# Three groups behind a layer norm: two corrected, the third on chunks normed in advance

## The chip, the cores and the metric

The kernel runs on one core of one Trainium2 chip. A core has a matrix engine (TensorE, PE in the profile), a vector engine (DVE), an activation engine (ACT), a general engine (POOL, GpSimd) and an engine that only issues transfers here (SP). Each works through its own list of instructions in order, and waits on semaphores for the others. The metric is device time in microseconds; lower is better.

## The reference, cut to what matters

Two layers transform a residual stream `h` of L = 272 rows (256 tokens and 16 meta rows) by D = 2048 features. Each layer is

```
proj = h @ w_in                      # q,k,v,gate for gated linear attention (GLA); q,k,v for neighbourhood attention
mix  = concat(gla(...), na(...)) @ w_out
h    = layer_norm(ALPHA * h + mix, ln1_w, ln1_b)
ff   = square(relu(h @ w_ff1)) @ w_ff2        # 2048 -> 8192 -> 2048
h    = layer_norm(ALPHA * h + ff, ln2_w, ln2_b)
layer_norm(x) = (x - mean) * rsqrt(var + eps) * gain + bias     # over the 2048 features of a row
```

The meta rows are dropped at the end, so the second layer needs only n = 256 rows behind its attention. Three norms are followed by a matrix product: the first norm of both layers (before `w_ff1`) and the second norm of layer 0 (before the `w_in` of layer 1, whose first columns are k and then v).

## The kernel before, in words

Activations lie transposed: 16 chunks `x[0..15]` of 128 features by L columns. Each chunk is a pair (high part, low part), two reduced-precision numbers that add up to the float; a product is then three matmuls: high weights by high x, high weights by low x, low weights by high x (`three`, lines 159 to 161). With n = 256 the first two are one matmul of 512 columns (lines 155 and 156).

Weights are streamed in tiles of 128 x 1024. `made` issues the transfer of a tile on SP into `raw`, casts it on ACT into `wh` (line 146) and subtracts on DVE into `wl` (line 147). All three have three buffers, and a tile is made one ahead of its use. One tile serves 8 chunks of one output of 128 features, or 2 chunks of four outputs.

A group is four outputs (512 columns of a weight matrix), that is eight tiles. `by_m` makes a group output by output: 16 chunks into one PSUM bank, then its evacuation. `by_k` makes it chunk by chunk: two chunks at a time into all four banks of the pool `pm`, so chunks may come late or may be overwritten behind it, but the four outputs end together. The host lays out the tiles of a group for one form or the other (`tiles`, `kinds`).

Behind a norm the mean and the scale of a row are known late. So `ln_add` writes into x the not yet normed value times the gain, and two more columns with gain and bias. A group on that x has n + 2 columns, and its sums are corrected by `fix` (lines 865 to 878): DVE copies the two extra sums out of PSUM (`wb`, line 874), subtracts mean times the gain's sum (line 875, which frees the bank), multiplies by the scale `rs` (line 876), and the evacuation adds the bias's sum as it applies its function. Meanwhile `ln_all` norms the accumulator `acc` itself, two chunks a step: two operations of DVE on both chunks (line 850, subtract and multiply), then gain and bias on POOL for each chunk (line 840). `renew` splits a normed chunk into x (lines 205 on ACT and 206 on DVE).

In the kernel before, both the first and the second group behind a norm are corrected. The first is `by_m`. The second is `by_k`, and behind each pair of chunks that it has used, `renew(k)` overwrites the pair before with normed values, for which it takes steps of `ln_all` where these are missing. From the third group on x is normed. In layer 0 and layer 1 the groups are the first two of `w_ff1`; between the layers they are k and v of layer 1.

Two queues of generators are worked off between the matmuls, by `pump(fg, bg)` after every 8 chunks: `fg` holds evacuations in pieces, `bg` holds `ln_all` (and GLA's heads). `NORMS = 0.4` is the number of `ln_all` steps a pump takes. A scheduler lays the instructions of each engine in one fixed order, in which such work is put behind the newest weight tile's `wl`.

The residual sum starts in `mixed`: POOL adds the two parts of each x chunk into `acc` (line 284) while the first group of `w_out` runs. In layer 1, v is evacuated by `ev_v` (line 362) and turned by three transposes (`v_rows`, line 371); the pool `early` that follows takes the memory of the norm's pools, and its first transfers (line 300 `wraw`, line 305 `wlr`) stand in SP's list among the weight tiles.

Of the kernel before, what the change touches and what calls it, by code (L numbers as in the profile page):

```python
# [14 lines left out]
P = 128  # L15
D = 2048
DC = D // P
# [14 lines left out]
EPS = 1e-5  # L32
TAU = 16.0
NEG = -1e30
GLA_R, GLA_NA, NORMS = 1.3, 1.1, 0.4


class Pair(tuple):
# [8 lines left out]
class Trunk:  # L47
# [138 lines left out]
                                      start=j + p == 0, stop=j == nk - 1 and p == 2)  # L186
        return [p[:, :n] for p in ps]

    def by_m(self, acts, ns, evict, pump=(0, 0), apart=False):

        nk = len(acts)
        for m, n in enumerate(ns):
            ps = self.pm.tile([P, 512], F32, name="mm", tag="mm")
            for k in range(nk):
                if k % 8 == 0:
                    wh, wl = self.weights()
                self.three(ps, wh, wl, (k % 8) * P, acts[k], n, k == 0, k == nk - 1)
                if k % 8 == 7 and k < nk - 1:
                    self.pump(*pump)
            parts = [ps[:, :T], ps[:, T:]] if n == T else [ps[:, :n]]  # L200
            evict(m, parts if apart else self.whole(parts))
            self.pump(*pump)
# [16 lines left out]
    def layer(self, l):  # L219
        nc, tc = self.nc, self.tc  # L220
        self.l = l
        self.full = l + 1 < DEPTH
        self.n = n = L if self.full else T
        with ExitStack() as actx:
            pool = lambda name, side, ctx=actx, bufs=1: ctx.enter_context(
                tc.tile_pool(name=name, bufs=bufs, side=side, reuse_waits="tile"))
            a = pool("att", "left")
            t = lambda nm, s: a.tile(s, F32, name=nm, tag=nm)
            self.qk = [t(f"qk{h}", [P, 2, L]) for h in range(GH)]
            self.be = [t(f"be{h}", [P, 2, L + 1]) for h in range(GH)]  # L230
            self.V = [t(f"V{i}", [P, GH * GDV]) for i in range(2)]
            self.VS = a.tile([80, GH * GDV], F32R, name="VS", tag="VS")
            nc.gpsimd.memset(self.VS.bitcast(F32), 0.0)
            self.y, self.gate, self.done = [None] * DC, {}, set()
            if l:
                self.by_m(self.x, [L + 2] * 4, lambda m, ps: self.fixed(self.ev_k, m, ps), pump=(1, NORMS))
                ps = self.by_k(self.x, L + 2, self.renew)
                self.renew(DC)
                for m in range(4):
                    self.fixed(self.ev_v, m, ps[m])  # L240
                self.drain()
                self.lctx.close()
            else:
                with ExitStack() as ectx:
                    self.xr = pool("xr", "right", ectx)
                    for m, ps in enumerate(self.by_k(self.x, L, self.load_x, fine=True)):
                        self.ev_k(m, ps)
            with ExitStack() as ectx:
                self.ep = pool("early", "right", ectx)
                self.fcredit = 0  # L250
                self.fg.append(self.gates())
                if l == 0:
                    self.by_m(self.x, [L] * 4, self.ev_v, pump=(1, 0))
                self.by_m(self.x, [n] * 4, self.ev_q, pump=(1, 0))
                self.by_m(self.x, [L] * 4, lambda m, ps: self.ev_v(4 + m, ps), pump=(1, 0))
                self.drain()
            self.a2 = pool("na", "left", bufs=2)
            with ExitStack() as gctx:
                self.credit = 0
                self.g2 = pool("gla", "right", gctx, 2)  # L260
                for h in range(GH):
                    self.bg.append(self.gla_head(h))
                for g in range(2):
                    self.by_m(self.x, [n] * 4, lambda m, ps: self.ev_r(4 * g + m, ps), pump=(1, GLA_R))
                self.na_tiles()
                for g in range(6):
                    if g == 5:
                        while self.bg:
                            self.step(self.bg, 1)
                        gctx.close()  # L270
                        self.ln_open()
                    ns = [n if (4 * g + m) % 3 == 0 else L for m in range(4)]
                    self.by_m(self.x, ns, lambda m, ps: self.ev_na(4 * g + m, ps), pump=(1, GLA_NA))
            ps = self.by_k(self.y, n, self.mixed)
            self.drain()
        self.tail(ps)

    def mixed(self, k):
        self.pump(1, 0)
        while not self.done.issuperset((k, k + 1)):  # L280
            self.step(self.fg, 1)
        for c in (k, k + 1):
            h, lo = (t[:, :self.n].bitcast(F32) for t in self.x[c])
            self.nc.gpsimd.tensor_tensor(self.acc[:, c, :self.n], h, lo, ALU.add)

    def load_x(self, k):
        nc = self.nc
# [68 lines left out]
    def ev_k(self, m, ps, **how):  # L356
        self.nc.scalar.activation(self.qk[m][:, 1, :], ps, AF.Identity, **how)

    def ev_v(self, c, ps, **how):
        pool, bufs = (self.l3, 3) if how else (self.ep, 2)  # L360
        vt = pool.tile([P, L], F32, name="ft", tag="ft", bufs=bufs)
        self.nc.scalar.activation(vt, ps, AF.Identity, **how)
        self.fg.append(self.v_rows(c, vt))

    def v_rows(self, c, vt):
# [296 lines left out]
    def tail(self, ps):  # L662
# [3 lines left out]
        with tc.tile_pool(name="u", bufs=1, reuse_waits="tile") as up:  # L666
# [6 lines left out]
            for half in range(2):  # L673
                u = [self.pair(self.yp, "y", k) if k < DC else self.pair(up, "u", k) for k in range(2 * DC)]

                def ev_f(k, ps, **how):
                    h, lo = u[k]
                    t = self.l3.tile([P, L], F32, name="ft", tag="ft")[:, :n]
                    if how or n > T:
                        nc.scalar.activation(t, ps, AF.Relu, **how)  # L680
                        nc.vector.tensor_tensor(t, t, t, ALU.mult)
                    else:
                        nc.vector.scalar_tensor_tensor(t, ps, 0.0, ps, ALU.max, ALU.mult)
                    self.split(t, h[:, :n], lo[:, :n])

                for g in range(8):
                    if half or g > 1:
                        self.by_m(self.x, [n] * 4, lambda m, ps: ev_f(4 * g + m, ps), pump=(1, 0))
                    elif g:
                        ps = self.by_k(self.x, n + 2, self.renew)  # L690
                        self.renew(DC)
                        for m in range(4):
                            self.fixed(ev_f, 4 + m, ps[m])
                        self.step(self.fg, 2)
                    else:
                        self.by_m(self.x, [n + 2] * 4, lambda m, ps: self.fixed(ev_f, m, ps), pump=(1, NORMS))

                def ev_2(m, ps, g):
                    k = 4 * g + m
                    a = acc[:, k, :n]  # L700
                    if half == 0:
                        nc.vector.scalar_tensor_tensor(a, a, ALPHA, ps[0], ALU.mult, ALU.add)
                        for part in ps[1:]:
                            nc.vector.tensor_tensor(a, a, part, ALU.add)
                    else:
                        self.ln_part(k, 1, ps)

                for g in range(4):
                    self.by_m(u, [n] * 4, lambda m, ps: ev_2(m, ps, g),
                              pump=(1, 0), apart=True)  # L710
# [102 lines left out]
    def ln_norm(self, which, l, n):  # L813
# [11 lines left out]
        nc.scalar.copy(mu, p1)  # L825
        nc.vector.tensor_tensor(var, p2, tn, ALU.subtract)
        end = self.newton(rs, var, self.eps, tn)
        self.norm = dict(mu=mu, rs=rs, last=end, n=n, ready=0, gb=[self.affine(l, which, k) for k in range(DC)])
        if not which or l < DEPTH - 1:
            self.bg.append(self.ln_all())  # L830
        yield
# [1 line left out]
    def ln_all(self):  # L833
        nc, acc, n = self.nc, self.acc, self.norm["n"]
        for k in range(0, DC, 2):
            self.ln_wide(k, 2, 0)
            self.ln_wide(k, 2, 1)
            for c in (k, k + 1):
                a, (gain, bias) = acc[:, c, :n], self.norm["gb"][c]
                nc.gpsimd.tensor_scalar(a, a, gain, bias, ALU.mult, ALU.add)  # L840
            self.norm["ready"] = k + 2
            yield

# [5 lines left out]
        by, alu = ((f["mu"], ALU.subtract), (f["rs"], ALU.mult))[op]  # L849
        return self.nc.vector.tensor_tensor(v, v, by[:, None, :].to_broadcast([P, m, n]), alu)  # L850

    def renew(self, k):

        f = self.norm
        n = f["n"]
        for c in (k - 2, k - 1) if k else ():
            while f["ready"] <= c:
                self.step(self.bg, 1)
            h, lo = self.x[c]
            self.split(self.acc[:, c, :n], h[:, :n], lo[:, :n])  # L860

    def fixed(self, evict, m, ps):
        self.fg.append(self.fix(evict, m, ps))
# [40 lines left out]
def layout(inputs):  # L904
# [28 lines left out]
    o["win"] = tiles(np.concatenate(cols, axis=2), ((0, 0), (1, 1)))  # L933
    o["wlr"] = lr.reshape(DEPTH, DC, P, 32).transpose(0, 2, 1, 3).reshape(DEPTH, P, 512)
    o["wout"] = tiles(a["w_out"], ((0, 0), (1, 0)))
    o["wff1"] = tiles(a["w_ff1"], ((0, 1), (1, 1)))
    o["wff2"] = tiles(a["w_ff2"], (), 2)
    wup = np.zeros((DEPTH, LRK, 2, GH * GDK), f)
    for s in range(0, 96, 32):
# [55 lines left out]
```

## Time and profile before

| | us |
|---|---|
| median of 3 runs (2457.91 to 2458.53) | 2458.18 |
| profiled execution | 2458.56 |
| its span | 2456.7 |
| PE busy in it | 2412.8 (98%) |
| DVE busy | 1581.8 (64%) |
| ACT busy | 1177.2 (48%) |
| POOL busy | 321.4 (13%) |

Matmuls overlap: a row of the timeline with 0.29 us is followed by the next after 0.127 us. What counts for the time is the distance of starts, and the idle time in brackets behind a row, with what ended it. PEclk is the granted clock of the matrix engine as a share of full speed.

### The profile page before, as it was taken

The numbers are of one execution on the slowest core, as the hardware profiler recorded it, in microseconds if no ns is written. First come the engines' busy times: TensorE is split into PE (matmuls) and PEld (weight loads), VectorE is DVE, ScalarE is ACT, GpSimd is POOL, SyncE is SP. The second block draws the span as 40 slices with busy tenths as digits, with TensorE's granted clock in tenths as the row PEclk, the third lists the DMA queues.
The fourth block names the chain that finished last, engine by engine and source line by source line (L and its number), as shares of the span: only waits on it lengthen the run. The fifth ranks groups of instructions, "written<-read, shape, count | busy, mean of one in ns | idle before, by whom it ended". The sixth has DMA issues, their size and how long they took to land.

```text
span 2456.7 us, 43382 instructions
## 1 busy us (share of the span) xinstructions
PE 2412.8 (98%) x17388; PEld 2261.3 (92%) x17388; DVE 1581.8 (64%) x2481; ACT 1177.2 (48%) x1938; POOL 321.4 (13%) x503
## 2 busy tenths in 40 slices
PE   9999999999999999999999999999899999999997
PEld 8999899999999999999998888898888888888886
DVE  6687777785544455546568787768866555666655
ACT  6555555454433344444446555555544333444443
POOL 1164340020000000000012444320300000000000
PEclk9999999999999999999999999999999999999998
DMA  7544444545555555555554444446465655555553
GB/s 239 162 135 144 137 136 155 174 153 176 176 173 177 174 174 178 172 175 175 174 184 149 147 152 154 134 155 198 152 192 188 189 188 187 185 187 188 187 189 129
DMA packets 118361, 417.25 MB, mean 170 GB/s; under 512 B 13388, under 2 KB 16460, under 8 KB 118160
## 3 DMA queue, kind: packets, MB, share of 16 engines
q1 hardware_dynamic: 118160, 414.49, 53.4%
q8 instruction: 136, 2.23, 0.4%
q14 instruction: 65, 0.53, 0.1%
HBM read 412.34 MB, written 2.10 MB: 169 GB/s over the span
## 4 chain that ended last, share of the span: by engine, by line
PE 92%; DVE 3%; POOL 2%; issue 1%; ACT 1%; DMA 0%; SPq 0%; ACTq 0%; POOLq 0%; DVEq 0%
PE mm L155 22%; PE mm L159 17%; PE mm L161 17%; PE mm L160 17%; PE mm L156 11%; PE mm L185 3%; POOL lev L455 1%; DVE acc L850 1%; POOL acc L840 1%; PE bg L490 1%; DVE wl L147 1%; PE bg L640 0%; PE bg L592 0%; PE bg L642 0%; ACT wh L146 0%
## 5 line engine op out<-in xcount | busy, mean ns | idle before, releaser
L147 DVE TENSOR_TENSOR wl<-raw,wh 128x1024 fp32r<-128x1024 f32 (+1 forms) x772 | 948.7, 1230 | 636.8 <-ACT wh L146 629.7
L146 ACT CAST wh<-raw 128x1024 fp32r<-128x1024 f32 (+1 forms) x772 | 806.2, 1045 | 944.3 <-PE mm L160 408.6
L159 PE MATMUL mm<-x,wh 128*128 128x272 f32 (+2 forms) x2112 | 615.4, 291 | 5.0 <-DVE wb L874 5.0
L161 PE MATMUL mm<-x,wl 128*128 128x272 f32 (+2 forms) x2112 | 610.5, 289 | 0.0
L160 PE MATMUL mm<-x,wh 128*128 128x272 f32 (+2 forms) x2112 | 610.3, 289 | 0.0
L155 PE MATMUL mm<-x,wh 128*128 128x512 f32 x1216 | 436.3, 400 | 10.6 <-DVE fx L875 10.6
L159 PEld LDWEIGHTS mm<-x,wh 128*128 128x128 f32 x2112 | 401.6, 190 | 9.6 <-ACT x L205 5.2
L161 PEld LDWEIGHTS mm<-x,wl 128*128 128x128 f32 x2112 | 398.8, 189 | 0.0
L160 PEld LDWEIGHTS mm<-x,wh 128*128 128x128 f32 x2112 | 398.2, 189 | 0.0
L156 PE MATMUL mm<-x,wl 128*128 128x256 f32 x1216 | 344.8, 284 | 1.0 <-DVE wl L147 1.0
L155 PEld LDWEIGHTS mm<-x,wh 128*128 128x128 f32 x1216 | 231.6, 190 | 66.2 <-ACT x L205 6.4
L155 PE MATMUL mm<-y,wh 128*128 128x512 f32 x704 | 247.9, 393 | 0.0
L156 PEld LDWEIGHTS mm<-x,wl 128*128 128x128 f32 x1216 | 231.5, 190 | 1.9 <-DVE wl L147 1.7
L161 PE MATMUL mm<-y,wl 128*128 128x272 f32 x704 | 203.1, 288 | 0.0
L159 PE MATMUL mm<-y,wh 128*128 128x272 f32 x704 | 203.0, 288 | 0.0
L160 PE MATMUL mm<-y,wh 128*128 128x272 f32 x704 | 202.7, 288 | 0.0
L156 PE MATMUL mm<-y,wl 128*128 128x256 f32 x704 | 197.5, 281 | 0.6 <-DVE wl L147 0.6
L155 PE MATMUL mm<-u,wh 128*128 128x512 f32 x512 | 180.6, 393 | 0.0
L455 POOL TENSOR_TENSOR lev<-be 128x128 f32<-128x128 f32 (+1 forms) x256 | 154.7, 634 | 143.7 <-PE bg L490 61.0
L155 PEld LDWEIGHTS mm<-y,wh 128*128 128x128 f32 x704 | 131.8, 188 | 30.1
L159 PE MATMUL mm<-u,wh 128*128 128x272 f32 x512 | 147.7, 288 | 0.0
L161 PE MATMUL mm<-u,wl 128*128 128x272 f32 x512 | 147.7, 288 | 0.0
(241 smaller groups left out, 3317.6 us busy)
## 6 DMA issues: line engine op xcount, KB each, us to landing
raw<-in_wff SPq DMA_DIRECT2D x512, 512.0 KB, 3.5
raw<-in_win SPq DMA_DIRECT2D x190, 512.0 KB, 3.6
raw<-in_wout SPq DMA_DIRECT2D x64, 512.0 KB, 3.6
nb<-in_nab SPq DMA_DIRECT2D x16, 352.0 KB, 3.2
out<-acc SPq DMA_DIRECT2D x8, 256.0 KB, 2.2
xraw<-in_xT SPq DMA_DIRECT2D x7, 272.0 KB, 5.4
wraw<-in_wup SPq DMA_DIRECT2D x2, 392.0 KB
raw<-in_win SPq DMA_DIRECT2D x4, 128.0 KB, 2.6
```

Source lines behind the costliest of these rows:

```text
L146: nc.scalar.copy(wh[:, c], raw[:, c])
L147: self.wl = nc.vector.tensor_tensor(wl[:, c], raw[:, c], wh[:, c].bitcast(F32), ALU.subtract).ins
L155: mm(ps, lhsT=wh[:, c:c + P], rhs=x.both[:, :, :T], start=first, stop=False)
L156: mm(ps[:, T:], lhsT=wl[:, c:c + P], rhs=xh[:, :T], start=False, stop=last)
L159: mm(o, lhsT=wh[:, c:c + P], rhs=xh[:, :n], start=first, stop=False)
L160: mm(o, lhsT=wh[:, c:c + P], rhs=xl[:, :n], start=False, stop=False)
L161: mm(o, lhsT=wl[:, c:c + P], rhs=xh[:, :n], start=False, stop=last)
L185: self.nc.tensor.matmul(ps[m][:, :n], lhsT=parts[p][0][:, c:c + P], rhs=acts[j][parts[p][1]][:, :n], start=j + p == 0, stop=j == nk - 1 an ...
L455: tt = lambda o, x, y: nc.gpsimd.tensor_tensor(o, x, y, ALU.subtract)
L490: nc.tensor.matmul(ps[b * 64:b * 64 + 64, s * 64:s * 64 + 64], lhsT=k[:, c:c + 64], rhs=q[:, r:r + 64], start=True, stop=True)
L840: nc.gpsimd.tensor_scalar(a, a, gain, bias, ALU.mult, ALU.add)
L850: return self.nc.vector.tensor_tensor(v, v, by[:, None, :].to_broadcast([P, m, n]), alu)
```

## The change

1. Behind each of the first norms of both layers, groups 0 and 1 of `w_ff1` are both `by_m` with corrected sums. `NORMS` becomes 0.6 there and 1.0 in front of k. At the middle of the last output before the third group, `renew(2)` norms the first two chunks.
2. Group 2 of `w_ff1` is `by_k` on normed x without the extra columns. Before each pair of chunks `normed(k)` takes one `fg` step and has chunks up to k + 4 split (`LEAD = 4`). Its four outputs are evacuated one a step through `later`. The host lays out group 2 for `by_k` instead of group 1.
3. Between the layers, k stays corrected and `by_m`; v becomes such a `by_k` on normed x with L columns instead of L + 2. Its outputs are evacuated after the norm's pools are closed, by plain copies on ACT, and their transposes go into the queue behind the decay gates instead of being run off before q.
4. `ln_all` gives gain and bias of the even chunks to ACT; the odd ones stay on POOL.
5. The corrected evacuation squares on ACT instead of DVE. Group 2 in layer 1 takes relu on ACT and the square on DVE, as layer 0 does.
6. `mixed` adds on DVE instead of POOL.

```diff
-GLA_R, GLA_NA, NORMS = 1.3, 1.1, 0.4
+GLA_R, GLA_NA, NORMS = 1.3, 1.1, (1.0, 0.6)
+LEAD = 4
...
+                if renew and m == len(ns) - 1 and k == 8:
+                    self.renew(2)
...
-                self.by_m(self.x, [L + 2] * 4, lambda m, ps: self.fixed(self.ev_k, m, ps), pump=(1, NORMS))
-                ps = self.by_k(self.x, L + 2, self.renew)
-                self.renew(DC)
-                for m in range(4):
-                    self.fixed(self.ev_v, m, ps[m])
+                self.by_m(self.x, [L + 2] * 4, lambda m, ps: self.fixed(self.ev_k, m, ps), pump=(1, NORMS[0]),
+                          renew=True)
+                first = self.by_k(self.x, L, self.normed)
                 self.drain()
                 self.lctx.close()
...
+                else:
+                    for m, ps in enumerate(first):
+                        self.ev_v(m, ps)
...
-            self.nc.gpsimd.tensor_tensor(self.acc[:, c, :self.n], h, lo, ALU.add)
+            self.nc.vector.tensor_tensor(self.acc[:, c, :self.n], h, lo, ALU.add)
...
-    def ev_v(self, c, ps, **how):
-        pool, bufs = (self.l3, 3) if how else (self.ep, 2)
-        vt = pool.tile([P, L], F32, name="ft", tag="ft", bufs=bufs)
-        self.nc.scalar.activation(vt, ps, AF.Identity, **how)
+    def ev_v(self, c, ps):
+        vt = self.ep.tile([P, L], F32, name="ft", tag="ft", bufs=4)
+        self.nc.scalar.copy(vt, ps)
...
-                    if how or n > T:
+                    if how:
                         nc.scalar.activation(t, ps, AF.Relu, **how)
+                        nc.scalar.activation(t, t, AF.Square)
+                    elif n > T or not half and 7 < k < 12:
+                        nc.scalar.activation(t, ps, AF.Relu)
                         nc.vector.tensor_tensor(t, t, t, ALU.mult)
...
-                    if half or g > 1:
+                    if half or g > 2:
                         self.by_m(self.x, [n] * 4, lambda m, ps: ev_f(4 * g + m, ps), pump=(1, 0))
-                    elif g:
-                        ps = self.by_k(self.x, n + 2, self.renew)
-                        self.renew(DC)
-                        for m in range(4):
-                            self.fixed(ev_f, 4 + m, ps[m])
-                        self.step(self.fg, 2)
+                    elif g == 2:
+                        ps = self.by_k(self.x, n, self.normed)
+                        self.fg.extend(self.later(ev_f, 8 + m, ps[m]) for m in range(4))
+                        self.step(self.fg, 1)
                     else:
-                        self.by_m(self.x, [n + 2] * 4, lambda m, ps: self.fixed(ev_f, m, ps), pump=(1, NORMS))
+                        self.by_m(self.x, [n + 2] * 4, lambda m, ps: self.fixed(ev_f, 4 * g + m, ps),
+                                  pump=(1, NORMS[1]), renew=g == 1)
...
-                nc.gpsimd.tensor_scalar(a, a, gain, bias, ALU.mult, ALU.add)
+                if c % 2:
+                    nc.gpsimd.tensor_scalar(a, a, gain, bias, ALU.mult, ALU.add)
+                else:
+                    nc.scalar.activation(a, a, AF.Identity, bias=bias, scale=gain)
...
-    def renew(self, k):
+    def normed(self, k):
+
+        self.pump(1, 0)
+        self.renew(min(DC, k + LEAD))
+
+    def renew(self, end):
 
         f = self.norm
         n = f["n"]
-        for c in (k - 2, k - 1) if k else ():
+        for c in range(f["new"], end):
             while f["ready"] <= c:
                 self.step(self.bg, 1)
             h, lo = self.x[c]
             self.split(self.acc[:, c, :n], h[:, :n], lo[:, :n])
+        f["new"] = end
+
+    def later(self, evict, m, ps):
+        evict(m, ps)
+        yield
...
-    o["wff1"] = tiles(a["w_ff1"], ((0, 1), (1, 1)))
+    o["wff1"] = tiles(a["w_ff1"], ((0, 2), (1, 2)))
```

More of the change, by code (lines that the diff above doesn't have):

```diff
@@ L187, in by_k, with by_m @@
         return [p[:, :n] for p in ps]
-    def by_m(self, acts, ns, evict, pump=(0, 0), apart=False):
+    def by_m(self, acts, ns, evict, pump=(0, 0), apart=False, renew=False):
         nk = len(acts)
@@ L827, in ln_norm @@
         end = self.newton(rs, var, self.eps, tn)
-        self.norm = dict(mu=mu, rs=rs, last=end, n=n, ready=0, gb=[self.affine(l, which, k) for k in range(DC)])
+        self.norm = dict(mu=mu, rs=rs, last=end, n=n, ready=0, new=0, gb=[self.affine(l, which, k) for k in range(DC)])
         if not which or l < DEPTH - 1:
```

## The prediction

> **What bounds the kernel now.** First the page's busy shares, then the view of waits for the matrix engine.
>
> ```profile
> span 2456.7 us, 43382 instructions
> ...
> PE 2412.8 (98%) x17388; PEld 2261.3 (92%) x17388; DVE 1581.8 (64%) x2481; ACT 1177.2 (48%) x1938; POOL 321.4 (13%) x503
> ```
> ```profile
> PE mm L155 <- DVE fx L875: 10.6, 2, 6.3
> PE mm L159 <- DVE wb L874: 5.0, 1, 5.0
> ```
>
> PE is busy for 98%, so only idle time and a lowered clock can be won. Three waits, 15.6 us together (10.6 + 5.0), end with the correction of an output, which frees a PSUM bank. Each lies at the end of the second corrected group, and the timeline of PE shows what each costs.
>
> ```profile
> 523.47 0.29 PE L185 MATMUL mm<-x,wh 128*128 128x274 f32 x1
> 528.77 0.56 PE L159 MATMUL mm<-x,wh 128*128 128x272 f32 x1 [5.02 <-DVE wb L874]
> ...
> 533.61 0.29 PE L159 MATMUL mm<-x,wh 128*128 128x272 f32 x1
> 533.74 0.29 PE L160 MATMUL mm<-x,wh 128*128 128x272 f32 x1
> ```
> ```profile
> 1304.61 0.29 PE L185 MATMUL mm<-x,wh 128*128 128x274 f32 x1
> 1309.21 0.77 PE L155 MATMUL mm<-x,wh 128*128 128x512 f32 x1 [4.32 <-DVE fx L875]
> ...
> 1316.16 0.39 PE L155 MATMUL mm<-x,wh 128*128 128x512 f32 x1
> ...
> 1317.09 0.49 PE L371 MATMUL bg<-ident,ft 128*128 128x128 f32 x3
> 1317.34 0.36 PE L156 MATMUL mm<-x,wl 128*128 128x256 f32 x1
> ...
> 1318.95 0.40 PE L155 MATMUL mm<-x,wh 128*128 128x512 f32 x1
> 1320.33 0.39 PE L156 MATMUL mm<-x,wl 128*128 128x256 f32 x1 [0.98 <-DVE wl L147]
> ```
> ```profile
> 1754.74 0.28 PE L185 MATMUL mm<-x,wh 128*128 128x258 f32 x1
> 1761.27 0.77 PE L155 MATMUL mm<-x,wh 128*128 128x512 f32 x1 [6.25 <-DVE fx L875]
> ...
> 1765.83 0.40 PE L155 MATMUL mm<-x,wh 128*128 128x512 f32 x1
> ...
> 1766.19 0.40 PE L155 MATMUL mm<-x,wh 128*128 128x512 f32 x1
> ...
> 1766.54 0.39 PE L155 MATMUL mm<-x,wh 128*128 128x512 f32 x1
> ```
>
> Behind each wait the starts are wider apart for a while: the granted clock is lower, as the windows show.
>
> ```profile
> 525.00:530.00 5.00, 1.23 (x5) 1.26 (x6) 4.20 (x11) 2.54 (x6) 3.55 (x4) 0.67 0.37 105
> ...
> 1310.00:1315.00 5.00, 5.00 (x18) 4.16 (x18) 3.86 (x14) 2.43 (x5) 0.03 (x1) 0.50 0.56 177
> ...
> 1320.00:1325.00 5.00, 4.67 (x31) 4.23 (x32) 4.67 (x7) 2.06 (x3) 0.00 (x0) 1.00 0.61 211
> ...
> 1760.00:1765.00 5.00, 3.73 (x11) 3.22 (x12) 4.51 (x12) 2.86 (x6) 1.16 (x2) 0.50 0.09 14
> ```
>
> The last three columns are the granted clock, the share of the transfer engines and GB/s. The clock is 0.50 to 0.67. So each place costs its wait and its slow stretch:
>
> - Layer 0, `w_ff1`: the next start was due at 523.47 + 0.13 = 523.60 and came at 528.77: 5.2. Then 21 matmuls took 4.84 (to 533.61) instead of 21 x 0.127 = 2.67: 2.2. Together 7.3.
> - Between the layers: due 1304.74, came 1309.21: 4.5. Up to 1316.16 there are 9 pairs of matmuls and three sets of transposes; at the later distances (0.352 a pair, 1766.19 to 1766.54; 0.25 a set, 1317.09 to 1317.34) that is 3.9, it took 6.95: 3.0. The row at 1320.33 came 1.38 behind its neighbour instead of two thirds of a pair, 0.24: 1.1. Together 8.6.
> - Layer 1, `w_ff1`: due 1754.86, came 1761.27: 6.4; 7 pairs in 4.56 instead of 2.46: 2.1. Together 8.5.
>
> Sum 24.4 us, all that can be won here. Why the bank comes late is seen in layer 0's second product:
>
> ```profile
> 1293.36 0.72 DVE L850 TENSOR_TENSOR acc<-acc,mu 128x544 f32<-128x544 f32 x1
> ...
> 1294.34 0.72 DVE L850 TENSOR_TENSOR acc<-acc,rs 128x544 f32<-128x544 f32 x1
> 1294.98 1.22 DVE L147 TENSOR_TENSOR wl<-raw,wh 128x1024 fp32r<-128x1024 f32 x1
> 1297.13 0.44 DVE L206 TENSOR_TENSOR x<-acc,x 128x272 fp32r<-128x272 f32 x1 [0.93 <-ACT x L205]
> 1297.49 0.72 DVE L850 TENSOR_TENSOR acc<-acc,mu 128x544 f32<-128x544 f32 x1
> ```
> ```profile
> 1295.23 1.96 POOL L840 TENSOR_SCALAR acc<-acc,vec 128x272 f32<-128x272 f32 x2 [2.17 <-DVE acc L850]
> ```
>
> Two chunks run through DVE, POOL, ACT and DVE again, one pair every 1297.49 - 1293.36 = 4.13 us, since DVE holds its list until ACT has split what POOL made. PE needs a pair every 24 x 0.127 = 3.05 us. The sums do not wait (they use x as it was), but the corrections stand behind this chain in DVE's list, and all four banks are taken.
>
> **The change part by part.** *Norming in the two corrected groups.* A pump now takes 0.6 or 1.0 steps of `ln_all`. In the instruction order of the changed program all eight steps of both first norms stand ahead of the first split of a chunk, and seven of eight between the layers; the eighth, for chunks 14 and 15 alone, stands ahead of the last tile's `wl`. The chain of 4.13 leaves the third group's path; its pairs need on DVE one `wl` and two splits, 1.22 + 2 x 0.44 = 2.1 of 3.05 us, and on ACT one cast and two splits.
>
> What hides the steps is DVE's free time under a corrected group of four outputs (192 matmuls x 0.127 = 24.4 us):
>
> ```profile
> 494.02 0.15 DVE L874 COPY wb<-mm 128x2 f32<-128x2 f32 x1
> 494.20 0.50 DVE L875 SCALAR_TENSOR_TENSOR fx<-mu,wb,mm 128x272 f32<-128x272 f32 x1
> ...
> 495.93 0.43 DVE L876 TENSOR_TENSOR fx<-fx,rs 128x272 f32<-128x272 f32 x1
> 496.95 0.44 DVE L681 TENSOR_TENSOR ft<-ft 128x272 f32<-128x272 f32 x1 [0.59 <-ACT ft L680]
> ```
> ```profile
> 538.51 0.38 ACT L680 ACTIVATE ft<-mm 128x272 f32<-128x272 f32 x1
> ```
>
> Eight `wl` x 1.22 = 9.8; four corrections with the low part (0.15 + 0.50 + 0.43 + 0.44) = 6.1; 8 pumps x 0.6 = 4.8 steps x 1.44 = 6.9. Sum 22.8 of 24.4: it fits, with the square (0.44 each) gone to ACT. I put 0.5 us for each of the two first norms, for DVE held up by an operand. In front of k it doesn't fit: 9.8 + 4 x 1.08 + 7 x 1.44 = 24.2, and the variance with Newton's three operations, of the corrections' size (0.43 to 0.50), comes ahead of all: 1.9 more, 26.1. Going down the list from the first norm operation, the `wl` of k's last tiles come just as PE needs them and that of v's second tile about 1 us late. Bounds: 0 if rows overlap as they do in the trace, 5 if DVE is as slow beside POOL as below; I take 2, nearer the list.
>
> Would so short a wait lower the clock too? The 0.98 us idle before 1320.33 left it at 1.00, 4.32 did not. Two us is nearer the first, so the sum takes nothing; a drop would add the 2.1 or 2.2 above. [...]
>
> *The third group's end.* Four banks end together again, but a plain evacuation frees one: relu on ACT, 0.38 (the row at 538.51).
>
> ```profile
> 1293.43 1.05 ACT L146 CAST wh<-raw 128x1024 fp32r<-128x1024 f32 x1
> ```
>
> In ACT's order two casts stand before it, the second for a buffer that comes free as the last pair begins; the cast and relu are done 1.05 + 0.38 = 1.4 us into a pair that lasts 3.05. Slack 1.6, cost 0. For v it is a plain copy, with room as well; what is then late next is its transposes: all four now stand behind the decay gates, six of eight at the end of v's second half, with four banks for them. I put 1 us there (0 to 2, two transposes waiting for a bank copied out by DVE and ACT). The transfers at 1310 (SP waiting for memory of the norm's pools) come earlier: the last use is now the split of chunk 15, before v ends, so the 1.1 above goes.
>
> *Matmul forms.* Group 2 of layer 1 has three matmuls of 256 for a pair of 512 and 256:
>
> ```profile
> 1638.19 0.28 PE L185 MATMUL mm<-y,wl 128*128 128x256 f32 x1
> ...
> 1638.54 0.28 PE L185 MATMUL mm<-y,wl 128*128 128x256 f32 x1
> ```
>
> 0.35 for three against 0.352 for the pair: 0. Two columns less for v: under 0.2, left out.
>
> *The residual sum on DVE.* 16 additions of 0.44 a layer, 7 us on DVE, under the last attention groups:
>
> ```profile
> 355.87 1.63 DVE L147 TENSOR_TENSOR wl<-raw,wh 128x1024 fp32r<-128x1024 f32 x1
> ```
> ```profile
> 369.00:372.00 3.00, 3.00 (x26) 3.00 (x25) 0.92 (x2) 2.29 (x10) 0.00 (x0) 1.00 0.33 131
> ```
>
> PE has no idle time there, DVE has (0.92 of 3), and without POOL beside it the `wl` needs 1.22, not 1.63. Cover gone, it would be 1 or 2 us a layer; with the lighter neighbour it may be less than nothing. I take 0 (-2 to +2).
>
> *The sum.* -24.4 + 1 (two first norms) + 2 (k and v) + 1 (transposes) = -20.4. Against the profiled execution (span 2456.7, 2458.56 in all) that is 2438.2; the median of the runs is 2458.18, 0.4 below it, hence 2438.
>
> **The rivals.** *DVE starved beside POOL.* POOL's half of `ln_all` now runs while DVE is full, and in the trace the two slow each other (1.63 for 1.22, 0.4 an operation). At worst every POOL operation holds DVE for its whole 0.98: 8 x 0.98 = 7.8 a norm, 3.9 a corrected group. Then `w_ff1` has 26.7 for 24.4, 4.6 a norm; k has 26.1 + 6.9 = 33 for 24.4, less one tile's lead of 3, 5.6. Cost 15 in place of 3: 2450. Two things speak against the full price: only half of the operations are left to POOL, and the row shows less than half of it. [...]
>
> *The evacuation is late again* (the change doesn't do what it says): if ACT is over 1.6 us behind at the end of the third group, the same bank is missing, and the three waits stay, with 4 us of new costs: 2462. The waits of before had the corrections behind the chain; nothing of it is left there.
>
> *Slower: the chain moves under PE.* The third group now reads the normed chunks, so where a pair needs longer than PE, PE waits itself. If it kept 4.13 for 3.05, three groups of eight pairs would lose 24 x 1.08 = 26, for 24.4 won and 4 paid: 2464. It decides from a pair of 3.9 us on. For it: the splits still go ACT, DVE in turn; against it: the steps stand before the group.
>
> **How the numbers follow.** My forecast 0.72, DVE starved 0.14, evacuation 0.07, the chain 0.07. A difference under 0.2% (4.9 us) can hardly be told from none. The forecast's own range is 2432 (the transposes, the residual sum and k free) to 2446; the starved case lies around 2450, up to 2454. The range 2432 to 2453 leaves out the last two and little more. Faster: 0.72, most of 0.14: 0.85. Same (2453.3 to 2463.1): the rest of it, the evacuation and a part of the chain: 0.09. Slower 0.06.
>
> **What would show it.** Right: no wait of PE over 2 us at the starts of group 3 of `w_ff1` and of q, PEclk 1.00 there, corrected groups of 24.4 us, POOL's norm operations all before the third group. Wrong: waits on `wl` in k or the second corrected group (starved), on x splits inside the third (chain), or on relu behind it (evacuation).

## The result, and the profile after

The changed kernel takes 2437.14 us (median of 4 runs, 2436.91 to 2437.55), the one before 2458.05 in the runs beside it: a ratio of 0.9917 with a 95% interval of 0.99 to 0.9934, so 20.9 us or 0.85% less. The forecast was 2438.

The page of the changed kernel, its first lines:

```profile
span 2435.6 us, 43411 instructions
...
PE 2407.7 (99%) x17452; PEld 2260.2 (93%) x17452; DVE 1574.8 (65%) x2481; ACT 1191.6 (49%) x1978; POOL 279.9 (11%) x447
```

PE has lost only 5 of its 2412.8 busy us, while the span has lost 21.1: what went was idle time (16.0) and slow clock. The view of waits for PE after the change (in total, how many, the longest):

```profile
PE mm L186 <- ACT wh L147: 4.7, 1, 4.7
PE bg L493 <- DVE lev L464: 1.6, 2, 1.3
PE mm L186 <- DVE wl L148: 1.0, 1, 1.0
```

The first is the start of the kernel. The 10.6 on `fx` and the 5.0 on `wb` are gone. PE's timeline at the three places (the end of the third group, L186, and the next group's first matmul):

```profile
547.62 0.29 PE L186 MATMUL mm<-x,wh 128*128 128x272 f32 x1
547.75 0.29 PE L160 MATMUL mm<-x,wh 128*128 128x272 f32 x1
...
1299.05 0.29 PE L186 MATMUL mm<-x,wh 128*128 128x272 f32 x1
1299.17 0.40 PE L156 MATMUL mm<-x,wh 128*128 128x512 f32 x1
...
1764.43 0.28 PE L186 MATMUL mm<-x,wh 128*128 128x256 f32 x1
1764.55 0.39 PE L156 MATMUL mm<-x,wh 128*128 128x512 f32 x1
```

The distance is 0.13, 0.12 and 0.12 us, that of two matmuls. The windows over the three groups (length; busy us of PE, PEld, DVE, ACT and POOL with instructions; granted clock; share of the transfer engines; GB/s):

```profile
523.00:548.00 25.00, 25.00 (x200) 25.00 (x199) 15.83 (x27) 13.12 (x24) 0.00 (x0) 1.00 0.54 169
1273.20:1299.15 25.95, 24.95 (x194) 24.37 (x193) 20.54 (x33) 12.79 (x20) 4.02 (x5) 1.00 0.66 189
1740.00:1765.00 25.00, 25.00 (x211) 24.96 (x210) 16.83 (x29) 14.22 (x28) 0.00 (x0) 1.00 0.57 189
```

The clock is full in all three. In the two `w_ff1` PE is busy throughout and POOL has nothing left. In v's group, the second row, PE is idle for 1.00 us (the wait for `wl` above), and POOL still works for 4.02 us, on the last four of its gains and one memset. So the sign that POOL's norm operations lie before the third group was met behind the first norms, and not in v.

To see where the time went, the span is cut at the first mean matmul of each norm (operand `onesr`), which stands at the same point of the work in every kernel: 480.38, 1261.53, 1714.08 and 2429.30 us before; 480.36, 1254.15, 1700.53 and 2407.95 after.

| stretch | before | after | difference | forecast |
|---|---|---|---|---|
| A, with `w_ff1` of layer 0 | 781.2 | 773.8 | -7.4 | -7.3 + 0.5 = -6.8 |
| B, with k and v of layer 1 | 452.6 | 446.4 | -6.2 | -8.6 + 2 + 1 = -5.6 |
| C, with `w_ff1` of layer 1 | 715.2 | 707.4 | -7.8 | -8.5 + 0.5 = -8.0 |

### The profile page after: what moved, and what is told of

The parts are those of the page before. It is cut to its first block, busy times and chain, and to the rows that moved or that the text cites. A ratio compares the mean times of both kernels' runs of the same rounds, so it can differ in the third digit from the quotient of the medians.

```text
span 2435.6 us, 43411 instructions
## 1 busy us (share of the span) xinstructions
PE 2407.7 (99%) x17452; PEld 2260.2 (93%) x17452; DVE 1574.8 (65%) x2481; ACT 1191.6 (49%) x1978; POOL 279.9 (11%) x447
## 4 chain that ended last, share of the span: by engine, by line
PE 94%; DVE 2%; POOL 1%; issue 1%; ACT 1%; DMA 0%; SPq 0%; ACTq 0%; POOLq 0%; DVEq 0%
PE mm L156 22%; PE mm L160 17%; PE mm L162 17%; PE mm L161 17%; PE mm L157 11%; PE mm L186 6%; POOL lev L458 1%; PE bg L493 1%; DVE acc L858 1%; DVE wl L148 1%; PE bg L643 0%; PE bg L595 0%; PE bg L645 0%; PE bg L323 0%; PE bg L536 0%
## 5 line engine op out<-in xcount | busy, mean ns | idle before, releaser
L160 PE MATMUL mm<-x,wh 128*128 128x272 f32 (+2 forms) x2176 | 632.7, 291 | 0.0
L161 PE MATMUL mm<-x,wh 128*128 128x272 f32 (+2 forms) x2176 | 627.8, 288 | 0.0
L162 PE MATMUL mm<-x,wl 128*128 128x272 f32 (+2 forms) x2176 | 627.6, 288 | 0.0
L156 PE MATMUL mm<-x,wh 128*128 128x512 f32 x1152 | 409.4, 397 | 0.0
L157 PE MATMUL mm<-x,wl 128*128 128x256 f32 x1152 | 324.5, 282 | 0.1
```

The lines of the kernel that those rows point to most:

```text
L156: mm(ps, lhsT=wh[:, c:c + P], rhs=x.both[:, :, :T], start=first, stop=False)
L157: mm(ps[:, T:], lhsT=wl[:, c:c + P], rhs=xh[:, :T], start=False, stop=last)
L160: mm(o, lhsT=wh[:, c:c + P], rhs=xh[:, :n], start=first, stop=False)
L161: mm(o, lhsT=wh[:, c:c + P], rhs=xl[:, :n], start=False, stop=False)
L162: mm(o, lhsT=wl[:, c:c + P], rhs=xh[:, :n], start=False, stop=last)
```

## The experiments

The letters are the stretches of that table. Times are medians; the kernel before took 2457.57, 2458.16 and 2458.46 in the three sets of runs.

**The chain, tried in the kernel before.** Only the split of gain and bias between POOL and ACT is put into the kernel before:

```diff
-                nc.gpsimd.tensor_scalar(a, a, gain, bias, ALU.mult, ALU.add)
+                if c % 2:
+                    nc.gpsimd.tensor_scalar(a, a, gain, bias, ALU.mult, ALU.add)
+                else:
+                    nc.scalar.activation(a, a, AF.Identity, bias=bias, scale=gain)
```

> The kernel before, with one part of the change alone: ACT takes gain and bias of the even chunks. My theory, that the chain of DVE, POOL, ACT and DVE makes the corrections late: its period falls from 4.13 us by one POOL operation (0.98) to 3.15, against PE's 3.05, so it ends hardly behind PE and the three waits fall from 5.0, 4.3 and 6.3 us to 1 or 2 each, without the slow clock behind them: about 15 of the 21 us are won, 2443. Rival, that four corrections ending together behind one group are the cause whatever the chain does: the waits stay above 4 us, less than 5 us are won, 2454 or more.

Measured 2454.82 (2453.44 to 2455.61), ratio 0.9988 (0.9978 to 0.9998): 2.7 us instead of the 14 or so that I expected. My expectation fell. The three waits stay:

```profile
PE mm L155 <- ACT x L205: 4.9, 1, 4.9
...
PE mm L159 <- ACT acc L843: 4.0, 1, 4.0
PE mm L155 <- DVE fx L878: 3.6, 1, 3.6
```

The timelines of the chain tell why. This kernel, one pair, DVE, POOL and ACT in turn:

```profile
510.74 1.22 DVE L147 TENSOR_TENSOR wl<-raw,wh 128x1024 fp32r<-128x1024 f32 x1
511.88 0.72 DVE L853 TENSOR_TENSOR acc<-acc,mu 128x544 f32<-128x544 f32 x1
512.51 0.44 DVE L206 TENSOR_TENSOR x<-acc,x 128x272 fp32r<-128x272 f32 x1
513.71 0.44 DVE L206 TENSOR_TENSOR x<-acc,x 128x272 fp32r<-128x272 f32 x1 [0.76 <-ACT x L205]
```
```profile
511.00 2.23 POOL L841 TENSOR_SCALAR acc<-acc,vec 128x272 f32<-128x272 f32 x1 [1.74 <-DVE acc L853]
```
```profile
513.26 0.42 ACT L205 CAST x<-acc 128x272 fp32r<-128x272 f32 x1 [1.32 <-POOL acc L841]
```

One POOL operation now takes 2.23, where two took 1.96 in the kernel before (the prediction's row at 1295.23; here, at 511.52, it is 1.96 too). The 0.98 I had read as the price of one was no price: the operation ended 0.28 us after DVE's list ran dry (512.51 + 0.44 = 512.95, then 513.23; times of POOL are rough, but ACT, which waits for this operation, starts at 513.26), while DVE's own `wl` kept its 1.22. So the pair repeats every 512.51 - 508.54 = 3.97 us (the split behind the norm's multiplication, the earlier one at 508.54) instead of 4.13, still far above PE's 3.05. Halving POOL's work hardly shortened the chain, and so this run neither confirms nor refutes that the chain is what makes the banks late. By its time it came out as the rival forecast (2454 or more); whether four corrections are the cause is taken up below, from the trace.

**The chain, moved under PE.** In the changed kernel the corrected groups pump no norm steps any more, so nearly all of the norm runs inside the third group:

```diff
-GLA_R, GLA_NA, NORMS = 1.3, 1.1, (1.0, 0.6)
+GLA_R, GLA_NA, NORMS = 1.3, 1.1, (0, 0)
```

> The changed kernel with no step of the norm taken by the pumps: all eight steps run where the third group calls for them, with ACT doing half of the gains. This is the rival of the chain under PE, made on purpose. If the chain bounds the third group: DVE alone has 1.22 + 0.88 + 1.44 = 3.5 us a pair, the chain of before 4.13, against 3.05 on PE; 24 pairs cost 12 to 26 us, 2449 to 2463, with PE waiting for x inside the third groups. If the steps are hidden there anyway: 2437 to 2440.

Measured 2464.38 (2463.94 to 2465.31), ratio 1.0026 (1.0014 to 1.0037): slower than before. A, B and C are 783.4, 453.9 and 717.5, that is 9.6, 7.5 and 10.0 above the changed kernel, 27.1 in all. The waits:

```profile
PE mm L186 <- ACT x L208: 21.3, 18, 2.5
```

DVE's splits in the third group of layer 0, one row a pair:

```profile
541.68 0.79 DVE L209 TENSOR_TENSOR x<-acc,x 128x272 fp32r<-128x272 f32 x2 [1.16 <-ACT x L208]
...
546.04 0.80 DVE L209 TENSOR_TENSOR x<-acc,x 128x272 fp32r<-128x272 f32 x2 [1.16 <-ACT x L208]
```

A pair takes 4.36 us where nothing but the chain holds it, and PE waits 18 times in the three groups of eight pairs. This is the prediction's slower rival brought about by an edit, at the 2464 that it named; its 24 x 1.08 = 26 measured 27.1. (Ahead of the kernel's end the clock was lowered once in it, for 3.41 us behind the longest wait, 2.53 us in layer 0.)

**Between the two.** The norm at 0.4 step a pump, the kernel before's value:

```diff
-GLA_R, GLA_NA, NORMS = 1.3, 1.1, (1.0, 0.6)
+GLA_R, GLA_NA, NORMS = 1.3, 1.1, (0.4, 0.4)
```

> The changed kernel with 0.4 steps a pump as before. Between the layers five of eight steps then fall into v's group, behind the first norms one or two into the third group. By the chain: five pairs late by 0.5 to 1.1 us, less the 0.97 us wait of v's second tile, and 0 to 1 us for each first norm: 2438 to 2442. If only the number of steps ahead of the third group's first chunk mattered, which is enough here: 2436.

Measured 2439.54 (2439.43 to 2439.65), ratio 0.9922 (0.9893 to 0.9951). The rest of the norm makes PE wait 2.4 us on x in three places; in return the wait for v's `wl` (0.97 after the change) is gone. What counts is that the steps come ahead of the third group, and 0.4 nearly does it.

**Only the two `w_ff1`.** k and v are again as before (v's sums by chunks, with the correction):

```diff
-                self.by_m(self.x, [L + 2] * 4, lambda m, ps: self.fixed(self.ev_k, m, ps), pump=(1, NORMS[0]),
-                          renew=True)
-                first = self.by_k(self.x, L, self.normed)
+                self.by_m(self.x, [L + 2] * 4, lambda m, ps: self.fixed(self.ev_k, m, ps), pump=(1, 0.4))
+                ps = self.by_k(self.x, L + 2, self.behind)
+                self.behind(DC)
+                for m in range(4):
+                    self.fixed(self.ev_v, m, ps[m])
```

(`behind` is the old `renew`; the evacuation and transposes of v are the old ones, and both of a pair's gains are on POOL as before.)

> The changed kernel with k and v made as before (0.4 steps, v on sums with a correction, gains on POOL), so that only the two places of w_ff1 are changed. If the three places are worth what they show each, independent of the others: from layer 0's second norm to layer 1's first 452.4 us as before instead of 446.4, 6.0 us more, 2443; the other two stretches as in the changed kernel. If the waits hang together (a lag handed on): more than 2 us away from that.

Measured 2443.57 (2443.29 to 2443.76), ratio 0.9939 (0.9924 to 0.9954), 6.5 above the changed kernel of the same set. A and C are 773.8 and 707.5 as after the change, B is 452.4 as before it, with its 4.3 on `fx` back. The places add up, and each place gains by its own part of the change.

**Parts undone in the changed kernel.** First, both gains of a pair on POOL again (the diff of the first experiment, reversed):

> The changed kernel with gain and bias of all chunks on POOL again. My theory, that the place of the norm's steps matters and not the engine: 8 more POOL operations a norm slow DVE by 0.4 each, 3 us of DVE a norm, which the first norms hold and k does not: 1 to 3 us more, 2439. Rival, that ACT's half is what brought the gain: the chunk chain of 1.96 us on POOL holds the third group, 8 us or more, 2445.

Measured 2439.96 (2438.5 to 2441.65), ratio 0.9928 (0.9913 to 0.9943): 2.8 us lost. A and C do not move (773.8, 707.0); B has 449.8, 3.4 more, and the first of PE's waits grew from 4.7:

```profile
PE mm L186 <- ACT wh L147: 6.5, 2, 4.4
```

The second of these two, 2.1 us at 1278.80, is v's second tile: ACT's cast stands behind splits that wait for POOL, up to 1.95 us each. It is 1.1 us longer than the 0.97 after the change. Behind it the granted clock was 0.50 from 1280.37 to 1283.78, which is up to 1.7 us more. ACT helps where DVE's list is full, and in these runs nowhere else.

Second, the square on DVE again, and third, the residual sum on POOL again:

```diff
-                        nc.scalar.activation(t, t, AF.Square)
+                        nc.vector.tensor_tensor(t, t, t, ALU.mult)
```

> The changed kernel with the squares of the corrected outputs on DVE again. My count: DVE has 22.8 us of work in a corrected group of 24.4, four squares of 0.44 bring it to 24.6, just over: 0 to 1 us a group at most where the rows overlap less than I think, 2438 in all (2437 to 2441). Rival, DVE is already at its limit there (held by POOL): each square shows in full, 16 x 0.44 = 7 us, 2444.

```diff
-            self.nc.vector.tensor_tensor(self.acc[:, c, :self.n], h, lo, ALU.add)
+            self.nc.gpsimd.tensor_tensor(self.acc[:, c, :self.n], h, lo, ALU.add)
```

> The changed kernel with the residual sum on POOL again. My term for this part was 0: 2437, within 1 us. Rival, that the lighter neighbour was worth something (or DVE's 7 us cost something): 2 us or more either way.

Measured 2436.86, ratio 0.9915 (0.99 to 0.993), and 2436.7, ratio 0.9914 (0.99 to 0.9929), against 2437.14: both edits are worth nothing. The square's 0.44 on DVE was free time there too, at least in `w_ff1`, where the corrected groups have room.

**How much room the evacuation has, and when the clock falls.** ACT makes idle copies ahead of the third group's relu: 8 and 10 of them in the two layers, then 12 and 15.

```diff
+                        jn = self.jp.tile([P, T], F32, name="jn", tag="jn")
+                        for _ in range((8, 10)[l]):
+                            nc.scalar.copy(jn, ps[0][:, :T])
                         self.fg.extend(self.later(ev_f, 8 + m, ps[m]) for m in range(4))
```

> The changed kernel with the evacuation of the third group of w_ff1 made late on purpose: ACT copies a part of the first bank 8 times (layer 0) and 10 times (layer 1) into a spare tile ahead of it. Six copies go before ACT's cast of the weight tile that waits for the end of the group, the rest after it. If the bank alone sets the start of group 3: idle time of 1.05 (cast) + 2 x 0.3 + 0.38 = 2.0 us in layer 0, and 2.7 with four copies in layer 1. If the clock holds through such waits: 2442 in all; if it falls as after 4.3 us: 2 us more at each, 2446. [...]

> The same with 12 copies in layer 0 and 15 in layer 1: six and nine behind the cast, idle time 1.05 + 1.8 + 0.4 = 3.3 and 1.05 + 2.7 + 0.4 = 4.2 us. If the clock falls after both: 2437 + 7.5 + 4.3 = 2449; after the longer alone: 2447; after neither: 2445. [...]

Measured 2444.6 and 2450.29 (one run each). PE's timeline with 8 and 10 copies, layer 0 and then layer 1:

```profile
547.70 0.29 PE L186 MATMUL mm<-x,wh 128*128 128x272 f32 x1
550.32 0.39 PE L160 MATMUL mm<-x,wh 128*128 128x272 f32 x1 [2.33 <-ACT ft L686]
...
551.44 0.42 PE L162 MATMUL mm<-x,wl 128*128 128x272 f32 x1
551.66 0.43 PE L160 MATMUL mm<-x,wh 128*128 128x272 f32 x1
...
554.61 0.40 PE L161 MATMUL mm<-x,wh 128*128 128x272 f32 x1
554.83 0.30 PE L162 MATMUL mm<-x,wl 128*128 128x272 f32 x1
...
1768.10 0.28 PE L186 MATMUL mm<-x,wh 128*128 128x256 f32 x1
1771.65 0.51 PE L156 MATMUL mm<-x,wh 128*128 128x512 f32 x1 [3.28 <-ACT ft L686]
```

With 12 and 15, layer 0 (in layer 1 the idle time was 5.29):

```profile
547.60 0.29 PE L186 MATMUL mm<-x,wh 128*128 128x272 f32 x1
551.83 0.60 PE L160 MATMUL mm<-x,wh 128*128 128x272 f32 x1 [3.94 <-ACT ft L686]
552.22 0.43 PE L161 MATMUL mm<-x,wh 128*128 128x272 f32 x1
552.44 0.43 PE L162 MATMUL mm<-x,wl 128*128 128x272 f32 x1
```

First the room. ACT's rows:

```profile
545.87 0.40 ACT L686 ACTIVATE ft<-mm 128x272 f32<-128x272 f32 x1
```
```profile
549.87 0.69 ACT L686 ACTIVATE ft<-mm 128x272 f32<-128x272 f32 x2
```

After the change (first row) the relu ends at 546.27 and PE wants the bank at 547.75: 1.48 us to spare. With 8 copies (second row) it starts 4.0 later, of which the last matmul's 547.70 for 547.62 takes 0.08, so PE should be 4.0 - 0.08 - 1.48 = 2.4 late; it was 550.32 - 547.70 - 0.13 = 2.5. The 8 copies came to 4.0 and not to the 3.0 that they take because one more cast of 1.05 got in ahead. So the room is real, and each us beyond it is a us of PE: the rival of the late evacuation has its mechanism here, and its threshold at 1.5 us.

Then the clock. After 2.33 us idle, eight matmuls came, behind a first distance of 0.23 at the usual 0.13 us, and then, from 551.44 to 554.83, fifteen at 3.39 / 15 = 0.226: 15 x 0.1 = 1.5 us more. After 3.28 us idle in layer 1 nothing fell: from 1772.12 on the distances were 0.35 a pair. After 3.94 us the first distances were already slow, 0.39 and 0.22, and after 5.29 us the clock was 0.50 as well. So A grew by 4.1 and 6.6 and C by 3.1 and 6.5; of the two answers the experiment was to tell apart (the clock holds or falls at about 2.3 to 3.3 us) neither came, but one in each layer of the first run. The windows of that run show what differs; they are cut where the trace records a change of the granted clock (551.42 and 554.83) and at the same distance from there on, 3.413 us by the changes named in the last section (columns as above):

```profile
548.00:551.42 3.42, 1.10 (x8) 1.10 (x9) 1.96 (x4) 3.01 (x8) 0.00 (x0) 1.00 0.50 156
551.42:554.83 3.41, 3.41 (x17) 3.41 (x16) 0.77 (x2) 0.29 (x1) 0.00 (x0) 0.50 0.47 159
...
1766.57:1769.98 3.41, 1.81 (x16) 1.60 (x14) 1.34 (x2) 3.25 (x9) 0.00 (x0) 1.00 0.63 205
1769.98:1773.40 3.42, 1.75 (x10) 1.52 (x10) 2.63 (x5) 2.55 (x8) 0.00 (x0) 1.00 0.55 168
```

The stop of 2.33 us lay inside one window, which PE used for 1.10 of 3.42 us, and the next window was slow. The longer stop of 3.28 us was split by the edge at 1769.98, 1.6 us on either side, and neither window was followed by a slow one (the next also has 1.00).

**The two small waits that are left.** The norm in front of k at 0.75 instead of 1.0:

```diff
-GLA_R, GLA_NA, NORMS = 1.3, 1.1, (1.0, 0.6)
+GLA_R, GLA_NA, NORMS = 1.3, 1.1, (0.75, 0.6)
```

> The changed kernel with 0.75 instead of 1.0 steps a pump in front of k, so that DVE has one or two steps less there (1.44 us each) and two fall into v's group, where DVE has free time. If DVE's list in front of k is what makes v's second weight tile late: the wait of 0.97 us goes, 1 us less than the changed kernel. If the steps come too late for v's last chunks instead: the same or 1 us more.

The changed kernel itself, run again beside it:

> The changed kernel once more, as the measure for the three beside it on the same chip: 2437.

And, on top of the 0.75, twice as many queued steps (transposes, gates) a pump under v's second half in layer 1:

```diff
-                self.by_m(self.x, [L] * 4, lambda m, ps: self.ev_v(4 + m, ps), pump=(1, 0))
+                self.by_m(self.x, [L] * 4, lambda m, ps: self.ev_v(4 + m, ps), pump=(1 + l, 0))
```

> As the last, and in layer 1 two steps a pump during the second half of v, so that six of eight transposes run between the matmuls instead of together at its end. The wait of 1.30 us on GLA's first operands behind them should go: about 2 us less than the changed kernel in all. If those operands are late for another reason (POOL's own chain): no more than the kernel with 0.75 steps.

Measured 2435.43 (2435.17 to 2435.69; ratio 0.9906, 0.9889 to 0.9922), 2437.05 (2436.4 to 2438.68; 0.9914, 0.9899 to 0.9929) and 2434.42 (2434.17 to 2435.14; 0.9903, 0.9888 to 0.9917). Against the changed kernel's B of 446.4 they have 445.4 and 443.4. PE's longest wait in the last, behind the start of the kernel:

```profile
PE bg L488 <- DVE lev L464: 1.2, 1, 1.2
```

The wait for v's `wl` and those on `lev` from DVE at L493 are gone; the 1.2 at L488 is the one that the kernel before had at its L485 (1.23). This version is 2.6 us faster than the changed kernel beside it, with ranges that do not touch, and the fastest that was run. The profiled execution of the changed kernel in this set (2438.68, its slowest) has a B of 447.7: the stop at L493 was 1.60 us there instead of 1.30, and behind it the granted clock was 0.50 from 1370.61 to 1374.02.

## Why the prediction was right

**The 24.4 us.** All three waits went with their slow stretches, and the two `w_ff1` show the sizes: A gained 7.4 of 7.3, C 7.8 of 8.5. In C, other runs in which nothing of it was changed had 707.0 to 707.5, so the 0.7 that is missing is hardly more than the spread.

**The first norms, 0.5 each.** Too dear for layer 0: nothing. DVE did its eight steps beside the corrections without a wait of PE, and still had room for the squares.

**k and v, 2.** The tile named was the one: v's second `wl` came late.

```profile
1278.38 0.77 PE L186 MATMUL mm<-x,wl 128*128 128x272 f32 x4 [0.97 <-DVE wl L148]
1278.99 0.68 PE L186 MATMUL mm<-x,wh 128*128 128x272 f32 x4
```

0.97 us against "about 1 us late", and the clock stayed at 1.00, as assumed. With the pump of 0.75 the stop is gone. There the same matmul as in the second row is

```profile
1276.93 1.18 PE L186 MATMUL mm<-x,wh 128*128 128x272 f32 x8
```

Counted from the norm's first mean matmul it comes after 24.84 us in the changed kernel (1254.15) and after 22.93 with 0.75 (1254.00): 1.9 us. So the 2 us were right in size, though the stop is only half of them; the other half is wider starts without a wait, in k (19.08 us up to v's first matmul, 18.78 with 0.75) and in v's first matmuls (1.48 us for eight, against 1.01). Of the 1.9 us B keeps 1.0, because a wait of 0.60 us for another `wl` comes up later, in q.

**The transposes, 1.** The waits at the decay gates sum to 0.27 + 1.30 + 0.26 after, where the kernel before had one of 1.23: 0.6 more. The stretch from the first matmul on `ws`, in q's group, to the last of these waits takes 72.5 us after (1307.60 to 1380.12) and 70.7 before (1323.00 to 1393.66). Of these 1.9 us, 1.0 is the work of v's first four sets of transposes (0.25 a set), which lie ahead of the stretch in the kernel before and inside it after the change, and a wait of 0.46 on `lr` has gone; 1.3 are left, the 0.6 of the waits and 0.7 without a wait, whose cause stays open. So the term was near: 1.3 for 1, as far as the stretch is the transposes' alone.

**The evacuation, 0.** Right: its room was put at 1.6 us, is 1.48 in the profile, and the idle copies moved PE by just what went beyond it.

**The residual sum and the square, 0.** Right to 0.5 us, by the two runs that undo them.

**The reason for the late bank.** This is the step with a gap. The prediction named the chain of 4.13 us a pair through DVE, POOL, ACT and DVE. That this chain holds a pair for over 4 us, and that PE pays for it where it must wait for the pairs, is shown (4.36 us, and 27.1 us for three groups). That the corrections of before came late for standing behind it is not: the run that was to shorten the chain left it at 3.97, as one operation on POOL took 2.23 us where two had taken 1.96. What stood in front of the corrections can be seen in DVE's list of the kernel before, at the first of the three waits. PE's last matmul of the group ended at 523.76:

```profile
525.61 0.98 DVE L850 TENSOR_TENSOR acc<-acc,rs 128x544 f32<-128x544 f32 x1
526.51 0.15 DVE L874 COPY wb<-mm 128x2 f32<-128x2 f32 x1
...
527.77 0.44 DVE L206 TENSOR_TENSOR x<-acc,x 128x272 fp32r<-128x272 f32 x1 [0.76 <-ACT x L205]
528.13 0.49 DVE L875 SCALAR_TENSOR_TENSOR fx<-mu,wb,mm 128x272 f32<-128x272 f32 x1
```

From 523.76 to 528.62 DVE spent 0.64 us on the correction of the first bank (`wb`, then `fx`); the rest went to the end of a `wl`, three norm operations and two splits, with a wait of 0.76 for ACT, all ahead of `fx` in the list. PE started at 528.77, before the second bank's `fx` (530.07). So four corrections ending together are not what PE waited for; one sufficed. That a shorter chain alone would have brought it in time is not shown: the change took away the chain and moved the corrections at the same time, and no run did one without the other. It remains the reading that fits.

**The rivals.** DVE starved beside POOL, at 2450: no. The rows show the opposite holder. POOL's timeline after the change:

```profile
497.95 2.46 POOL L846 TENSOR_SCALAR acc<-acc,vec 128x272 f32<-128x272 f32 x1 [1.85 <-ACT wh L147]
...
506.37 0.57 POOL L846 TENSOR_SCALAR acc<-acc,vec 128x272 f32<-128x272 f32 x1 [3.57 <-ACT wh L147]
...
1262.41 12.75 POOL L846 TENSOR_SCALAR acc<-acc,vec 128x272 f32<-128x272 f32 x6 [12.52 <-DVE acc L858]
```

DVE's rows beside the first two:

```profile
497.92 1.23 DVE L148 TENSOR_TENSOR wl<-raw,wh 128x1024 fp32r<-128x1024 f32 x1
...
499.70 0.43 DVE L209 TENSOR_TENSOR y<-ft,y 128x272 fp32r<-128x272 f32 x1
500.05 0.15 DVE L892 COPY wb<-mm 128x2 f32<-128x2 f32 x1
...
506.30 0.50 DVE L893 SCALAR_TENSOR_TENSOR fx<-mu,wb,mm 128x272 f32<-128x272 f32 x1
```

The same POOL operation takes 2.46 us where DVE goes from `wl` to the split and ends (500.41) just behind the copy out of PSUM (`mm`); it takes 0.57 beside a correction that reads PSUM; and 12.75 / 6 = 2.1 during k, where DVE has no gap. DVE's `wl` there takes 1.21 to 1.43. It is POOL's operation that grows, as far as its rough times tell: the one of 2.46 us ends 0.21 us behind that copy (500.20), the one of 2.23 in the first experiment 0.28 us behind the end of DVE's list. The price of this rival, DVE held for all of POOL's 0.98, was my estimate, and no run shows it: a full DVE list nearly kept its pace, with those 1.21 to 1.43 us for a `wl` that takes 1.22 in the prediction's rows. What makes the two hold each other up is not shown. The evacuation that is late again, at 2462, and the chain under PE, at 2464, did not happen by themselves; runs that force them show both mechanisms, the second at its price.

**The clock.** The prediction took nothing for a stop of about 2 us, as nearer to 0.98 than to 4.32. For the 0.97 that came this held, and that is in part luck: where v's second tile was 2.10 us late (all gains on POOL), the clock was lowered behind it, and so it was behind a stop of 1.60 at L493. To judge by length was wrong: 1.60, 2.10 and 2.33 us idle were followed by a fall, 3.28 by none. The kernel before has a stop between the two as well, 1.23 us at L485 (PE starts again at 1393.66), and the clock was 1.00 behind it.

## What to carry to other kernels

A stage is best taken off the critical path by making its results one stage earlier, under work that does not need them; the price is then counted in the list of the engine that makes them, operand by operand (here one tile's `wl` and what led up to it, 2 us). Before an operation is moved off an engine, look at whether its row is work or waiting: POOL's 0.98 was half of a row of two, one operation alone took 2.23 us, and halving the work changed little (the pair went from 4.13 to 3.97 us). And pump such work neither too late (0: 27 us lost) nor too early (1.0: 1.6 us lost against 0.75).

## What the runs showed of the hardware that was not expected

- Beside DVE's `wl`, a norm operation, a split and the copy of `wb`, a POOL operation of 128x272 took 2.46 us, beside a `fx`, which reads `mm`, 0.57; one of the six during k took 3.9 (POOL's times are rough). DVE itself lost little beside those six (1.21 to 1.43 for its `wl`).
- The length of an idle time alone did not tell whether PE's clock fell: behind stops of 1.60 (the changed kernel run again), 2.10 (all gains on POOL) and 2.33 us (8 copies) it was 0.50, behind stops of 1.23 (the kernel before) and 3.28 us (10 copies) 1.00. The changes of the granted clock that are named here lie whole multiples of 3.413 us apart within a run. In the kernel before the slow stretches last from 526.70 to 533.53, from 1308.36 to 1315.18 and from 1758.91 to 1765.74, 6.83 us each, which is twice 3.413, and a fourth begins at 2441.58; the 774.83, 443.73 and 675.84 us between them are 227, 130 and 198 times 3.413. With 12 and 15 copies the two slow stretches end at 557.18 and 1779.15 (1221.97 / 358 = 3.413), with 8 and 10 copies the one lasts from 551.42 to 554.83. What sets these times is not shown.
- If the kernel before is cut at these changes and every 3.413 us from there, then behind its start four pieces at full clock had PE idle for 0.65 of their length or more: 0.87 (from 523.29), 1.00 (1304.94), 1.00 (1755.50) and 0.65 (2438.17). Each was followed by a slow one. All others at full clock were idle for 0.36 or less, and none was. A slow piece idle for 0.61, 0.25 or 0.69 (526.70, 1308.36, 1758.91) was followed by another slow one, one idle for 0.00 by a full one. The runs with copies agree: 0.68 (the window from 548.00 above), and 0.72 and 1.00 with 12 and 15 copies, were followed by a slow piece, 0.47 and 0.49 (from 1766.57 and 1769.98) by a full one. Near 0.47 the share is no sure sign: the stop of 1.60 us, behind which the clock fell, is by itself 0.47 of 3.413. Idle is here what the profile shows as such for PE.
